# Keys of the first backward pass in two places of their own, and the first blocks of the projection in another order

## The chip, the cores and the metric

The kernel runs on one core of one Trainium2 chip. The metric is device time in microseconds (us). The kernel before took 2343.8 us, the median of three runs (2341.11 to 2347.96). The shares of busy time, the waits and the rows of the timeline come from one profiled execution of it.

The engines are called as in the profile: PE does the matmuls, PEld loads their stationary operand, DVE, ACT and POOL are the three engines that work on elements, SP issues the DMAs.

## The reference

One encoder layer on `x` of 2048 tokens by 1024 channels, all in float32. Cut to its steps:

```python
h = rms_norm(x, norm_pre_g)
proj = h @ w_in                       # 9232 columns
u_a, z_a, q, k, v, o, z_b, gates, g_a, g_b = split(proj)
pooled = multiscale_pool(u_a)         # branch A: windows 2, 4, 8, 16
y_a = (pooled @ pool_mix_w) * pool_scale * silu(z_a)
q, k = split(silu(centred_depthwise_conv(concat(q, k), conv_qk_w, conv_qk_b)))
...
# branch B: mLSTM, 4 heads of 256, both directions, chunks of 128 tokens
kw = kc * exp(w_end - m_chunk)        # weighted keys of one chunk
c_chunk = kw^T v                      # what the chunk adds to the state
c_new = keep * c_st + add * c_add     # the state, chunk after chunk
num = (q k^T * d) v + inter_scale * (q c_prev)
...
merged = sigmoid(g_a) * (y_a @ w_proj_pool) + sigmoid(g_b) * (y_b @ w_proj_mlstm)
out = x + rms_norm(merged @ w_out, norm_post_g)
```

## The kernel before

**Precision.** Nearly every matrix product is made of three matmuls (L110 to L112): each operand is split into a high part (`Copy` to the matmul's type on ACT, L98) and a low part (operand minus high part, on POOL or DVE, L102). The names end in `h` and `l`. `put` (L198) does that for a part of x, `prep_w` (L417) for a pair of blocks of weights.

**Phase 1** (L511) is the input projection, kept transposed: x in two halves of 1024 tokens, the columns of `w_in` in pairs of 2 x 128. For half 0, x is read as eight quarters `X[q]` of 128 x 2 x 512, scaled by the norm, and combined into the seven left operands of Strassen's scheme: A11, A12, A22 as they are, and S1 to S4, which `combos` (L206) makes from the four blocks a11, a12, a21, a22 **in place** (S1 lies where a22 was, S3 where a21 was, S2 where a11 was, S4 where a12 was). `operands` (L221) picks the room of each quarter (L227): `raw` and `acc` are rooms for working copies of the columns, `wc` is the pool of ten rooms in which the split blocks of weights lie, so two of those blocks (`wB`, `wT`) can be written only when the quarters in their rooms have been split.

The first two pairs of half 0 are made the plain way ("quarters", L500 to L502, 8 chunks of 128 channels, three matmuls each) while `combos` runs. Pair 2 is the first by Strassen's scheme (L443), in this order on PE: A11·B11 (bank A), S2·T2 (bank B), S1·T1 (bank C), S3·T3 (bank B again), A22·T4 and so on; T1 to T4 are sums of weight blocks. `u2` (L469) is bank B plus bank A's copy; S3·T3 goes into the same bank and so must wait for it. Between the products stand steps of other work: `pair_g` (L828) puts a sigmoid on a finished bank (`sg`, L841, ACT), `gates` (L658) sums the 16 gate columns and copies them out (`gsb`, L671, ACT), and `fps` (L373) are small matmuls that fold a weight of branch A.

**Ties.** The order on each engine is made by a scheduler from the order of the program and priorities. `tc.issue_after(x)` is a tie by hand: what is made under it stands behind `x` in the order. `prep_w` of pair 2 is tied so to `self.scaled[8]`.

**Fill-in matmuls.** `busy` (L277) is a matmul whose result nobody reads: one ahead of the sums of squares (`ssqp`, L258), one behind the broadcast of the norm's factor (`rbp`, L183).

**mLSTM** starts right behind phase 1. The first pass runs backwards over head 0: for the 16 chunks, `back1` (L1304) transposes the keys (`kt` on PE, L1311, copied to `kn` by ACT, L1314), `keys` (L1260) weighs them, and `update` (L1249) makes 15 states: two products `cu` of three matmuls (L1040 to L1042) per state, and on DVE the new state `cb` = old state times keep plus `cu` (L1256; the first is a copy by ACT, L1254). For the first pass alone the weighted keys take a way of their own: ACT makes `kw` (L1267) in a room of the pool `w1` (8 rooms, which otherwise carries weights of the output), DVE rounds it to the high part (CAST, L1268), POOL subtracts (L1269). All other passes use `weigh` (L1242): ACT writes the high part (L1244), DVE the low one in one instruction (L1245), in `KB` = 2 rooms per direction in the pool `io`. Behind each state the first outputs follow: `s` = q·k (L1374), its weights `dm` = Exp (L1377, ACT), `sd`, `qs`, and `num` (L1401 to L1406). Exp needs another table of functions in ACT than phase 1 uses; `none` (L1274) is an Exp of one column whose result nobody reads.

After that the passes of the heads, branch A, branch B and the output follow; nothing of the change lies there.

Of the kernel before, what the change touches and what calls it, by code (L numbers as in the profile page):

```python
# [8 lines left out]
F32 = mybir.dt.float32  # L9
F32R = mybir.dt.float32r  # L10
# [3 lines left out]
P = 128  # L14
# [67 lines left out]
class Kernel:  # L82
# [123 lines left out]
    def combos(self, H, j, a11, a12, a21, a22):  # L206

        nc = self.nc
        s1, s3, s2, s4 = a22, a21, a11, a12
        nc.vector.tensor_tensor(s1, a21, a22, op=ALU.add)  # L210
        nc.vector.tensor_tensor(s3, a11, a21, op=ALU.subtract)
        nc.vector.tensor_tensor(s2, s1, a11, op=ALU.subtract)
        self.put(H, "S2", j, s2, "act", "dve")
        self.put(H, "S1", j, s1, "act", "pool")
        self.put(H, "S3", j, s3, "act", "pool")
        return lambda: (
            nc.vector.tensor_tensor(s4, a12, s2, op=ALU.subtract),
            self.put(H, "S4", j, s4, "act", "dve"),
        )

    def operands(self, half, H, hp, wc, pool, psum):  # L221
# [5 lines left out]
        for b, q, where in ((0, 0, "raw"), (0, 2, "acc"), (0, 1, "acc"), (0, 3, "acc"), (1, 0, "raw"), (1, 2, "raw"), (1, 1, wc), (1, 3, wc)):  # L227
            if where is wc:
                t = wc.tile([P, 2, BLK], F32, tag="wc", name=self.nm("xT"))
            else:  # L230
                t = pool.tile([P, 2, BLK], F32, tag=where, name=self.nm("xT"))
            room[b, q] = t
# [15 lines left out]
        def sums():  # L248
# [8 lines left out]
            for i in range(4):  # L257
                nc.tensor.matmul(ps[:, i : i + 1], acc[:, i * P : (i + 1) * P], self.one_c, start=True, stop=True)  # L258
            busy(X[7][0][:, :P], X[7][0])
# [3 lines left out]
            busy(self.rstd[:, :1].to_broadcast([P, P]), X[7][0])  # L263
# [59 lines left out]
        ends = [self.combos(H, j, X[j][0], X[4 + j][0], X[j][1], X[4 + j][1]) for j in range(4)]  # L323
# [187 lines left out]
    def phase1(self):  # L511
        tc, nc, a = self.tc, self.nc, self.a
        with ExitStack() as es:
# [25 lines left out]
            for half in range(2):  # L539
# [53 lines left out]
                for i in range(2, n):  # L593
# [7 lines left out]
                    with tc.high_priority(offset=200):  # L601
                        if half == 0:
                            with tc.issue_after(self.scaled[8].ins) if i == 2 else ExitStack():
                                self.prep_w(W, load(i), wc, wt)
# [53 lines left out]
    def gates(self, half, H, W, psum, pool):  # L658
        nc = self.nc
        for b in range(2):  # L660
# [10 lines left out]
            nc.scalar.activation(g, ps, AF.Copy)  # L671
# [550 lines left out]
    def mlstm(self, turns, ends):  # L1222
        nc, tc, sp, col = self.nc, self.tc, self.sp, self.cols
        E = DH + 2
        with ExitStack() as es:
# [16 lines left out]
            def weigh(out, k, w):  # L1242

                nc.scalar.activation(out[0], k, AF.Copy, scale=w)  # L1244
                nc.vector.scalar_tensor_tensor(  # L1245
                    out[1], k, w, out[0].bitcast(F32), op0=ALU.mult, op1=ALU.subtract
                )

# [11 lines left out]
            def keys(h, c, d):  # L1260

                if d == 1 and h == 0:

                    kw = self.w1.tile([P, 2, 512], F32, tag="w", name=self.nm("kw"))[:, 0, :DH]
                    k = self.w1.tile([P, 2, 512], F32R, tag="w", name=self.nm("k"))
                    out = k[:, 0, :DH], k[:, 1, :DH]
                    up = nc.scalar.activation(kw, kn[h, c // 4][:, c % 4, :], AF.Copy, scale=col["w"][:, ix(d, h, c)])  # L1267
                    nc.vector.tensor_copy(out[0], kw)  # L1268
                    nc.gpsimd.tensor_tensor(out[1], kw, out[0].bitcast(F32), op=ALU.subtract)  # L1269
                    if c == NC_ // 2:  # L1270

                        none = last.tile([P, 1], F32, tag="none", name="none", bufs=1)
                        with tc.issue_after(up.ins):
                            nc.scalar.activation(none, self.one_c, AF.Exp)  # L1274
                    return out
                out = split2(io, [P, DH], f"k{d}", bufs=KB)
                weigh(out, kn[h, c // 4][:, c % 4, :], col["w"][:, ix(d, h, c)])
                return out
# [384 lines left out]
    def tail(self):  # L1663

        tc = self.tc
        with ExitStack() as es:
            w1 = self.w1 = es.enter_context(tc.tile_pool(name="w1", bufs=8, side="right", reuse_waits="tile"))
# [96 lines left out]
```

## Time and profile before

| | us |
|---|---|
| median of three runs | 2343.8 |
| the profiled execution | 2344.1 |
| its span, first to last instruction | 2342.3 |
| PE busy | 2285.9 (98% of the span) |
| mean granted TensorE clock | 0.993 |
| DVE / POOL / ACT busy | 1412.6 / 1184.2 / 885.8 |

Some 1.8 us of the profiled execution lie outside the span. PE is busy for nearly all of it and at the full clock nearly always, so what a change here can move is found by going through the stretches in which PE idles or has a lower clock, not by the shares of the whole. The busy time is of PE's matmuls, which overlap: the distance from start to start is the better measure of their rate.

### The profile page before, as it was taken

How to read it: one execution, taken by the hardware profiler on the slowest of the kernel's cores; microseconds unless marked ns; L12 is line 12 of the kernel's file. 1: busy time of each engine (PE TensorE's matmuls, PEld its weight loads, DVE VectorE, ACT ScalarE, POOL GpSimd, SP SyncE). 2: the span in 40 equal slices, each digit the busy share in tenths (PEclk: the TensorE clock that was granted, in tenths of full speed). 3: DMA queues.
4: the chain of work that ended last, by engine and by line, in shares of the span. 5: the costliest groups of instructions: out<-in, count | busy, mean ns of one | idle time of the engine just before them, and what ended most of it. 6: DMA issues, size and time to landing. Idle time of an engine off the chain costs nothing. (4 is left out here: it accounts for less than half of the span.)

```text
span 2342.3 us, 32965 instructions
## 1 busy us (share of the span) xinstructions
PE 2285.9 (98%) x11545; PEld 1938.1 (83%) x11545; DVE 1412.6 (60%) x2379; ACT 885.8 (38%) x1796; POOL 1184.2 (51%) x917
## 2 busy tenths in 40 slices
PE   7899999999999999999999999899999999999998
PEld 5788888888888788888878788699998888999886
DVE  6665656768765555546656565388887453454365
ACT  5334333333343423323333233467766221111342
POOL 4755545666664533356564555245556341233574
PEclk9999999999999999999999999899999999999999
DMA  5567766766685366788888787767767696677863
GB/s 211 188 237 271 259 222 223 265 234 219 222 296 206 110 203 212 228 297 279 295 298 287 265 299 270 258 193 246 238 190 243 219 321 227 214 277 256 329 207 126
DMA packets 233270, 564.43 MB, mean 241 GB/s; under 512 B 23568, under 2 KB 70800, under 8 KB 233104
## 3 DMA queue, kind: packets, MB, share of 16 engines
q1 hardware_dynamic: 233104, 562.33, 69.7%
q8 instruction: 91, 1.49, 0.3%
q14 instruction: 75, 0.61, 0.1%
HBM read 340.46 MB, written 221.77 MB: 240 GB/s over the span
## 5 line engine op out<-in xcount | busy, mean ns | idle before, releaser
L102 POOL TENSOR_TENSOR wB<-wraw,wB 128x512 fp32r<-128x512 f32 x220 | 333.1, 1518 | 293.3 <-ACT wB L98 232.7
L98 ACT ACTIVATE wB<-wraw 128x512 fp32r<-128x512 f32 x224 | 139.3, 626 | 268.7 <-PE bankB L112 121.9
L102 POOL TENSOR_TENSOR wT<-wt,wT 128x512 fp32r<-128x512 f32 x102 | 148.5, 1459 | 128.2 <-ACT wT L98 105.5
L718 DVE SCALAR_TENSOR_TENSOR acc<-raw,conv_w,acc 128x1026 f32<-128x1026 f32 (+1 forms) x96 | 151.2, 1587 | 10.5 <-ACT acc L713 9.7
L1040 PE MATMUL pb<-oxs,w_proj_mlstm 128*128 128x256 f32 x512 | 143.9, 281 | 0.7 <-DVE sga L1206 0.4
L1042 PE MATMUL pb<-oxs,w_proj_mlstm 128*128 128x256 f32 x512 | 143.9, 281 | 0.0
L1041 PE MATMUL pb<-oxs,w_proj_mlstm 128*128 128x256 f32 x512 | 143.8, 281 | 0.0
L98 ACT ACTIVATE wT<-wt 128x512 fp32r<-128x512 f32 x136 | 85.3, 629 | 153.5 <-PE bankB L112 60.4
L1385 POOL TENSOR_TENSOR qs<-q,isc 128x256 f32<-128x256 f32 x120 | 90.0, 754 | 93.1 <-PE num L1401 59.9
L110 PE MATMUL bankB<-S3h,wT 128*128 128x512 f32 x272 | 106.2, 390 | 3.6 <-DVE u L469 3.6
L110 PE MATMUL bankB<-A22h,wT 128*128 128x512 f32 x272 | 106.1, 390 | 2.1 <-DVE u L474 2.1
L110 PE MATMUL bankA<-A12h,wB 128*128 128x512 f32 x272 | 108.0, 397 | 0.0
L110 PE MATMUL bankC<-S4h,wB 128*128 128x512 f32 x272 | 106.2, 391 | 1.2 <-DVE raw L685 1.2
L112 PE MATMUL bankA<-A11h,wB 128*128 128x512 f32 x272 | 106.0, 390 | 1.3 <-POOL wB L102 1.3
L1025 POOL TENSOR_TENSOR nm<-nm,mask 128x256 f32<-128x256 f32 x64 | 60.4, 955 | 91.4 <-DMA nm<-negM 74.2
L111 PE MATMUL bankB<-S2l,wT 128*128 128x512 f32 x272 | 106.5, 392 | 0.0
L110 PE MATMUL bankC<-S1h,wT 128*128 128x512 f32 x272 | 106.4, 391 | 0.0
L111 PE MATMUL bankC<-S4l,wB 128*128 128x512 f32 x272 | 106.4, 391 | 0.0
L112 PE MATMUL bankA<-A12h,wB 128*128 128x512 f32 x272 | 106.2, 391 | 0.0
L110 PE MATMUL bankA<-A11h,wB 128*128 128x512 f32 x272 | 106.2, 390 | 0.0
L111 PE MATMUL bankA<-A12l,wB 128*128 128x512 f32 x272 | 106.1, 390 | 0.0
L112 PE MATMUL bankC<-S4h,wB 128*128 128x512 f32 x272 | 106.1, 390 | 0.0
(417 smaller groups left out, 7097.3 us busy)
## 6 DMA issues: line engine op xcount, KB each, us to landing
wt<-wT SPq DMA_DIRECT2D x136, 512.0 KB, 4.4
wT<-wt SPq DMA_DIRECT2D x136, 512.0 KB, 6.0
wraw<-in_w_in SPq DMA_DIRECT2D x98, 512.0 KB, 5.2
vh<-vnh SPq DMA_DIRECT2D x16, 516.0 KB, 4.4
vl<-vnl SPq DMA_DIRECT2D x16, 516.0 KB, 5.7
v<-vh SPq DMA_DIRECT2D x16, 516.0 KB, 8.8
v<-vl SPq DMA_DIRECT2D x16, 516.0 KB, 8.5
xT<-in_xT SPq DMA_DIRECT2D x16, 512.0 KB, 6.5
```

What stands on the lines that cost most here:

```text
L98: self.upper = nc.scalar.activation(hi, x, AF.Copy)
L102: return eng.tensor_tensor(lo, x, hi.bitcast(F32), op=ALU.subtract)
L110: nc.tensor.matmul(ps, wh, xh, start=start and kt == 0, stop=False, skip_group_check=True)
L111: nc.tensor.matmul(ps, wh, xl, start=False, stop=False, skip_group_check=True)
L112: end = nc.tensor.matmul(ps, wl, xh, start=False, stop=stop and kt == 3, skip_group_check=True)
L718: nc.vector.scalar_tensor_tensor(acc[:, :n], raw[:, tap : tap + n], self.cw[:, ct, tap : tap + 1], acc[:, :n], op0=ALU.mult, op1=ALU.add,)
L1025: nc.gpsimd.tensor_tensor(t[:, d, :, :], t[:, d, :, :], mask[:, d, None, :].to_broadcast([P, 2, P]), op=ALU.add)
L1040: nc.tensor.matmul(ps, wh, xh, start=i == 0, stop=False)
L1041: nc.tensor.matmul(ps, wh, xl, start=False, stop=False)
L1042: nc.tensor.matmul(ps, wl, xh, start=False, stop=i == n)
L1385: nc.gpsimd.tensor_tensor(qs[d], q[:, :, ck], isc[:, d, j % 2, None, :].to_broadcast([P, 2, P]), op=ALU.mult)
```

## The change

Three things at the start, two in the middle.

1. The rooms of the quarters of x: quarter (1,1), a half of a21, goes to a room `raw`, and quarter (1,2), a half of a22, to a room `wc` (before the other way round). Both rooms `wc` now hold a22, which becomes S1; before, one of them held a half of a21, which becomes S3. The low part of S1 of half 0 is made by DVE in place of POOL (4 instructions).
2. Fill-in matmuls: the first is tied behind the four `ssqp` and there are two behind `rbp` instead of one.
3. `prep_w` of pair 3 is tied behind the last `sg` and behind `gsb`.
4. The first pass's keys go through `weigh` like all others, in the two rooms of direction 1; the rooms in `w1`, the 15 CASTs on DVE and the 15 subtractions on POOL are gone, 15 `scalar_tensor_tensor` on DVE come in.
5. The Exp without a reader is tied, as before, behind the weighing of chunk 8.

```diff
-    def combos(self, H, j, a11, a12, a21, a22):
+    def combos(self, H, j, a11, a12, a21, a22, le):
...
-        self.put(H, "S1", j, s1, "act", "pool")
+        self.put(H, "S1", j, s1, "act", le)
...
-        for b, q, where in ((0, 0, "raw"), ..., (1, 0, "raw"), (1, 2, "raw"), (1, 1, wc), (1, 3, wc)):
+        for b, q, where in ((0, 0, "raw"), ..., (1, 0, "raw"), (1, 1, "raw"), (1, 2, wc), (1, 3, wc)):
...
-                nc.tensor.matmul(ps[:, i : i + 1], acc[:, i * P : (i + 1) * P], self.one_c, start=True, stop=True)
-            busy(X[7][0][:, :P], X[7][0])
+                done = nc.tensor.matmul(
+                    ps[:, i : i + 1], acc[:, i * P : (i + 1) * P], self.one_c, start=True, stop=True
+                )
+            with tc.issue_after(done.ins):
+                busy(X[7][0][:, :P], X[7][0])
...
-            busy(self.rstd[:, :1].to_broadcast([P, P]), X[7][0])
+            for _ in range(2):
+                busy(self.rstd[:, :1].to_broadcast([P, P]), X[7][0])
...
-        ends = [self.combos(H, j, X[j][0], X[4 + j][0], X[j][1], X[4 + j][1]) for j in range(4)]
+        ends = [self.combos(H, j, X[j][0], X[4 + j][0], X[j][1], X[4 + j][1], ("dve", "pool")[half]) for j in range(4)]
...
-                            with tc.issue_after(self.scaled[8].ins) if i == 2 else ExitStack():
+                            ties = [self.scaled[8]] if i == 2 else [self.evac, self.gated] if i == 3 else []
+                            with ExitStack() as behind:
+                                for t in ties:
+                                    behind.enter_context(tc.issue_after(t.ins))
                                 self.prep_w(W, load(i), wc, wt)
...
-            nc.scalar.activation(g, ps, AF.Copy)
+            self.gated = nc.scalar.activation(g, ps, AF.Copy)
...
             def keys(h, c, d):
-                if d == 1 and h == 0:
-                    kw = self.w1.tile([P, 2, 512], F32, tag="w", name=self.nm("kw"))[:, 0, :DH]
-                    k = self.w1.tile([P, 2, 512], F32R, tag="w", name=self.nm("k"))
-                    out = k[:, 0, :DH], k[:, 1, :DH]
-                    up = nc.scalar.activation(kw, kn[h, c // 4][:, c % 4, :], AF.Copy, scale=col["w"][:, ix(d, h, c)])
-                    nc.vector.tensor_copy(out[0], kw)
-                    nc.gpsimd.tensor_tensor(out[1], kw, out[0].bitcast(F32), op=ALU.subtract)
-                    if c == NC_ // 2:
-                        none = last.tile([P, 1], F32, tag="none", name="none", bufs=1)
-                        with tc.issue_after(up.ins):
-                            nc.scalar.activation(none, self.one_c, AF.Exp)
-                    return out
                 out = split2(io, [P, DH], f"k{d}", bufs=KB)
-                weigh(out, kn[h, c // 4][:, c % 4, :], col["w"][:, ix(d, h, c)])
+                up = weigh(out, kn[h, c // 4][:, c % 4, :], col["w"][:, ix(d, h, c)])
+                if (h, c, d) == (0, NC_ // 2, 1):
+                    none = last.tile([P, 1], F32, tag="none", name="none", bufs=1)
+                    with tc.issue_after(up.ins):
+                        nc.scalar.activation(none, self.one_c, AF.Exp)
                 return out
```

Line numbers of the kernel after run up to 8 higher from L281 on, and one lower behind `keys`; the rows below have their own.

PE's first rows, at the start of the program: `ssqp` are the sums of squares, `rbp` the broadcast, `bankA` and `bankB` the first products. Before:

```order
L281 MATMUL busy_352<-xT_310 128x512
L258 MATMUL ssqp_347<-one_c,sq_344 128x1 x4
L183 MATMUL rbp_357<-ident,rstd 128x128 x4
L281 MATMUL busy_363<-xT_310,rstd 128x512
L500 MATMUL bankA_504<-A11h_406,wB_35_394 128x512
```

And now:

```order
L258 MATMUL ssqp_347<-one_c,sq_344 128x1 x4
L285 MATMUL busy_352<-xT_310 128x512
L183 MATMUL rbp_357<-ident,rstd 128x128 x4
L285 MATMUL busy_363<-xT_310,rstd 128x512
L285 MATMUL busy_365<-xT_310,rstd 128x512
L504 MATMUL bankA_506<-A11h_408,wB_36_396 128x512
```

The first `busy` moved behind the four `ssqp`, and one more stands ahead of the first product.

ACT's rows in the middle of pair 2, from the last weights of pair 2 (`wT_94` and `wB_95` before) over the sigmoids of pair 1 to the copy of pair 2's first product (`p`); `wB_110` to `wB_117` are weights of pair 3. Before:

```order
L98 ACTIVATE wT_94_850<-wt_848 128x512
L98 ACTIVATE wB_95_853<-wraw_825 128x512
L841 ACTIVATE sg_781<-bankC_636,b_merge 128x512
L98 ACTIVATE wB_110_956<-wraw_952 128x512
L841 ACTIVATE sg_784<-bankC_637,b_merge 128x512
L98 ACTIVATE wT_113_963<-wt_961 128x512
L841 ACTIVATE sg_793<-bankA_644,b_merge 128x512
L98 ACTIVATE wT_114_966<-wt_959 128x512
L841 ACTIVATE sg_796<-bankB_645,b_merge 128x512
L671 ACTIVATE gsb_801<-gps_688 32x512
L98 ACTIVATE wT_116_971<-wt_969 128x512
L463 ACTIVATE p_101_877<-bankA_862 128x512
```

And now:

```order
L98 ACTIVATE wT_95_852<-wt_850 128x512
L98 ACTIVATE wB_96_855<-wraw_827 128x512
L848 ACTIVATE sg_783<-bankC_638,b_merge 128x512
L848 ACTIVATE sg_786<-bankC_639,b_merge 128x512
L848 ACTIVATE sg_795<-bankA_646,b_merge 128x512
L848 ACTIVATE sg_798<-bankB_647,b_merge 128x512
L678 ACTIVATE gsb_803<-gps_690 32x512
L98 ACTIVATE wB_111_958<-wraw_954 128x512
L98 ACTIVATE wT_114_965<-wt_963 128x512
L98 ACTIVATE wT_115_968<-wt_961 128x512
L98 ACTIVATE wT_117_973<-wt_971 128x512
L467 ACTIVATE p_102_879<-bankA_864 128x512
```

The four `sg` and `gsb` stand together ahead of pair 3's weights, between which they stood.

ACT's rows at the first pass, from the copies of the transposed keys (`kn`) on; `k` is a high part from `weigh`, `kw` the weighted key of the old way, `cb` the first state. Before, from the copies of the last whole group of four chunks:

```order
L1314 ACTIVATE kn_12081<-kt_12126 128x256
L1314 ACTIVATE kn_12081<-kt_12146 128x256
L1244 ACTIVATE k_1845_12202<-kn_12081,col_w 128x256
L1244 ACTIVATE k_1853_12221<-kn_12081,col_w 128x256
L1314 ACTIVATE kn_12163<-kt_12164 128x256
L1244 ACTIVATE k_1831_12168<-kn_12163,col_w 128x256
L1267 ACTIVATE kw_11838<-kn_11833,col_w 128x256
L1267 ACTIVATE kw_11847<-kn_11833,col_w 128x256
L1267 ACTIVATE kw_11867<-kn_11833,col_w 128x256
L1267 ACTIVATE kw_11887<-kn_11833,col_w 128x256
L1267 ACTIVATE kw_11910<-kn_11905,col_w 128x256
L1254 ACTIVATE cb_11852<-cu_11853 128x258
```

And now, from the last sigmoid of phase 1 (`u`):

```order
L848 ACTIVATE u_1717_11689<-u_1717_11689,b_merge 128x512
L1313 ACTIVATE kn_11835<-kt_11836 128x256
L1313 ACTIVATE kn_11835<-kt_11844 128x256
L1251 ACTIVATE k_1727_11840<-kn_11835,col_w 128x256
L1251 ACTIVATE k_1730_11848<-kn_11835,col_w 128x256
L1313 ACTIVATE kn_11835<-kt_11863 128x256
L1313 ACTIVATE kn_11835<-kt_11882 128x256
L1251 ACTIVATE k_1736_11867<-kn_11835,col_w 128x256
L1262 ACTIVATE cb_11852<-cu_11853 128x258
L1262 ACTIVATE cb_11852<-cu_11858 128x258
```

The weighing of the first chunk stood behind the copies of all 17 transposes and now stands behind two; the copies of later chunks come between the steps of the pass. On PE the first `cu` stood behind 17 `kt` in the same way and now stands behind four, and the first `s` stands behind the last `cu` of the pass, where before it stood behind the ninth. The load of Exp's table (before: ahead of the first `dm`) stands behind the key of chunk 8, the eighth of the 15.

More of the change, by code (lines that the diff above doesn't have):

```diff
@@ L226, in operands @@
         room = {}
-        for b, q, where in ((0, 0, "raw"), (0, 2, "acc"), (0, 1, "acc"), (0, 3, "acc"), (1, 0, "raw"), (1, 2, "raw"), (1, 1, wc), (1, 3, wc)):
+        for b, q, where in ((0, 0, "raw"), (0, 2, "acc"), (0, 1, "acc"), (0, 3, "acc"), (1, 0, "raw"), (1, 1, "raw"), (1, 2, wc), (1, 3, wc)):
             if where is wc:
@@ L1242, in weigh @@
             def weigh(out, k, w):
-                nc.scalar.activation(out[0], k, AF.Copy, scale=w)
+                up = nc.scalar.activation(out[0], k, AF.Copy, scale=w)
                 nc.vector.scalar_tensor_tensor(
@@ L1247, in weigh @@
                 )
+                return up
             def update(new, kw, v, old, keep):
@@ L1666, in tail @@
         with ExitStack() as es:
-            w1 = self.w1 = es.enter_context(tc.tile_pool(name="w1", bufs=8, side="right", reuse_waits="tile"))
+            w1 = es.enter_context(tc.tile_pool(name="w1", bufs=8, side="right", reuse_waits="tile"))
             self.kv = es.enter_context(tc.tile_pool(name="kv", bufs=KV, reuse_waits="tile"))
```

## Prediction

> **What bounds the kernel now.** I read the page's first part, then one table of windows over the whole span, then PE's waits in the two stretches that the table points to, then the timeline there.
>
> ```profile
> PE 2285.9 (98%) x11545; PEld 1938.1 (83%) x11545; DVE 1412.6 (60%) x2379; ACT 885.8 (38%) x1796; POOL 1184.2 (51%) x917
> ...
> core 0: us, PE busy (x) PEld busy (x) DVE busy (x) ACT busy (x) POOL busy (x), PEclk, DMA share, GB/s
> 0.00:20.40 20.40, 7.72 (x20) 4.49 (x20) 9.79 (x42) 10.44 (x17) 4.12 (x7) 1.00 0.92 318
> 20.40:24.90 4.50, 4.47 (x11) 3.51 (x12) 4.50 (x6) 3.48 (x10) 2.11 (x2) 1.00 1.02 415
> 24.90:74.90 50.00, 50.00 (x225) 38.85 (x223) 35.65 (x47) 24.45 (x47) 37.24 (x19) 1.00 0.22 80
> 74.90:95.70 20.80, 13.88 (x53) 10.85 (x52) 15.10 (x13) 11.66 (x23) 16.09 (x11) 0.84 0.78 273
> ...
> 1492.20:1508.20 16.00, 8.22 (x35) 4.74 (x33) 2.26 (x5) 9.02 (x23) 0.00 (x0) 0.62 1.04 410
> 1508.20:1516.50 8.30, 7.24 (x31) 6.95 (x32) 6.02 (x13) 7.22 (x18) 7.12 (x10) 0.50 0.76 265
> 1516.50:1532.00 15.50, 13.70 (x99) 12.54 (x99) 13.41 (x37) 6.23 (x15) 8.28 (x12) 1.00 0.85 295
> ```
>
> PE is the bound wherever it is full, as from 24.9 on: 50.00 of 50.00 us, 225 matmuls, one every 0.222 us. It is not full, or not at that rate, in three places: up to 24.9 (in 20.40 to 24.90 eleven matmuls in 4.5 us), from 74.9 to 95.7 (13.88 us busy of 20.8, clock 0.84), and at the first pass from 1492.2 to 1516.5 (clock 0.62, then 0.50) and on to 1532. All that the change touches lies there. Who ends PE's waits stands in brackets in the rows below.
>
> **The start, fill-in matmuls.** PE's timeline at the first products:
>
> ```profile
> 15.37 2.08 PE L183 MATMUL rbp<-ident,rstd 128*128 128x128 f32 x8 [1.74 <-POOL rstd L161]
> 17.24 1.91 PE L281 MATMUL busy<-xT,rstd 128*128 128x512 f32 x2
> 20.43 0.79 PE L500 MATMUL bankA<-A11h,wB 128*128 128x512 f32 x1 [1.27 <-ACT A11h L98]
> ```
>
> The eleven matmuls from 20.43 on start some 0.43 us apart (4.5 over 10.5), those after 24.9 every 0.222. That is ten at 0.21 us too much: **2.1 us of half clock** (the PEclk column, 1.00 there, doesn't show it; the count does). The change moves the first `busy` (1.9 us) into the hole ahead of `rbp` (15.37, a wait of 1.74) and adds one behind it, from 19.15 to about 21 at half clock, sooner if the clock has risen. PE is then busy with hardly a hole from 11.8 to 20.4, which is longer than the 4.5 us that it took from 20.43 on to bring the clock up. **Gain 2.1 us, bounds 0 and 2.1** (nothing, where fill-in work does not raise the clock; and an extra `busy` that ends at 21.0 instead of 20.43 would take 0.6 of it). The factor that `rbp` feeds comes through ACT and isn't touched.
>
> **The start, low half of S1 on DVE.** POOL's and DVE's rows while the plain pairs run, and what PE met behind them:
>
> ```profile
> 52.89 2.49 DVE L210 TENSOR_TENSOR xT<-xT,xT 128x512 f32<-128x512 f32 x4
> ...
> 54.32 14.99 POOL L102 TENSOR_TENSOR S1l<-xT,S1h 128x512 fp32r<-128x512 f32 x4 [3.71 <-ACT S1h L98]
> 69.27 5.95 POOL L102 TENSOR_TENSOR S3l<-xT,S3h 128x512 fp32r<-128x512 f32 x4
> 75.19 1.26 POOL L102 TENSOR_TENSOR wB<-wraw,wB 128x512 fp32r<-128x512 f32 x1
> ...
> 74.75 0.40 PE L111 MATMUL bankA<-A11l,wB 128*128 128x512 f32 x1
> 76.50 0.50 PE L112 MATMUL bankA<-A11h,wB 128*128 128x512 f32 x1 [1.34 <-POOL wB L102]
> ...
> 81.64 1.89 PE L373 MATMUL fps<-fm,fw 128*128 128x256 f32 x8
> 89.11 3.78 PE L373 MATMUL fps<-fm,fw 128*128 128x256 f32 x8 [5.57 <-ACT gsb L671]
> ```
>
> DVE's 19 instructions from 52.89 on take 0.60 us each (four in 2.49 with their overlap), without a hole to 64.4. POOL's four S1l took 15 us in the same time, where four S3l take 5.95: POOL hardly gets in while DVE runs so. Now DVE's stream has 25 instructions (4 S1l, the last S2l and one more come in): 52.9 + 25 x 0.60 = 68.0. POOL has only S3l: held up to 68.0, then 4 x 1.25 = 5 us, to 72.9, then the low part of B11 to 74.2 against 76.45 before. PE wants it at 74.97 (0.22 behind 74.75) and got on at 76.50. So this 1.5 us goes, by a margin of 0.8 us.
>
> Then `gsb`, ACT's last of a chain: the difference for T4 on DVE, its wT, wB, and four `sg` with three weights of pair 3 between them, one of which waited for DVE:
>
> ```profile
> 79.87 1.77 DVE L426 TENSOR_TENSOR wt<-wraw,wt 128x512 f32<-128x512 f32 x1
> ...
> 81.67 0.63 ACT L98 ACTIVATE wT<-wt 128x512 fp32r<-128x512 f32 x1 [3.18 <-DVE wt L426]
> ...
> 86.29 0.63 ACT L98 ACTIVATE wT<-wt 128x512 fp32r<-128x512 f32 x1 [1.79 <-DVE wt L426]
> ...
> 88.48 0.57 ACT L671 ACTIVATE gsb<-gps 32x512 f32<-32x512 f32 x1
> ```
>
> The tie puts these five together, 5 x 0.57 us behind wT and wB. The T4 difference needs T1's low part, POOL's next instruction behind B11's, so 74.2 + 1.2 = 75.4; at 1.7 us, as at 79.87 where DVE and POOL meet, it ends near 77, wT and wB near 78.1, `gsb` near **80.9**. PE reached the first `fps` at 81.64; without the 1.5 us it is there at 80.1 and at the second at 82.0. So the 5.57 us wait goes too, by a margin of 1 us, and with it the 8 `fps` at half clock (3.78 for 1.89) and the first S1·T1 at half clock.
>
> **What is late next.** S3·T3 must wait for `u2`, which stands on DVE behind differences for pairs 3 and 4:
>
> ```profile
> 85.67 0.33 SPq L346 DMA_DIRECT2D wraw<-in_w_in  x1
> ...
> 94.18 0.69 DVE L426 TENSOR_TENSOR wt<-wraw,wt 128x512 f32<-128x512 f32 x1 [2.19 <-DMA wraw<-in_w_in]
> 94.79 0.68 DVE L469 TENSOR_TENSOR u<-bankB,p 128x512 f32<-128x512 f32 x1
> ...
> 95.69 0.40 PE L110 MATMUL bankB<-S3h,wT 128*128 128x512 f32 x1
> ```
>
> Before, `u2` ended at 95.47 and bound nothing by much. Now PE wants S3·T3 at 82.0 + 1.89 + 2.7 (twelve products) = 86.6. From 52.9 on DVE and POOL have 36 and 12 instructions up to `u2`; where they exclude each other, that is 36 x 0.60 + 12 x 1.2 = 36 us, to 89.0, with `u2` near 89.7; the raw weight that stands ahead of it (94.18) was asked for at 85.67, behind POOL's weights of pair 2, and is now asked for some 3.5 us sooner. So a **new wait of about 3.1 us**, and S3·T3 starts at 89.7 against 95.69: **gain 6.0, bounds 4 and 9** (`u2` at 92, or no wait). Behind it the order is as before, and PE is full.
>
> Whether the clock survives that wait is open by these rows: a wait of 1.74 us at 1326 kept it (next starts 0.34 and 0.24 apart), one of 3.93 at 1226 lost it:
>
> ```profile
> 1230.13 1.76 PE L744 MATMUL vtr<-ident,raw 128*128 128x128 f32 x7 [3.93 <-DVE raw L685]
> ...
> 1327.75 0.50 PE L110 MATMUL bankB<-S3h,wT 128*128 128x512 f32 x1 [1.74 <-DVE u L469]
> ```
>
> Lost, it costs as at 20.43, 2.1 us. I take it as kept, since 1.4 above the kept one and 0.8 under the lost one leave it open, and give the other case to rival (1).
>
> The Trainium skill, page "TensorE: Matmul & The Clock Gate", section "Part 1: The HAM clock gate", has the clock fall after an idle window of about 3.4 us that runs free, and rise after as much of steady work. By that a wait of 3.1 us keeps the clock, and one of 3.5 loses it, and the sum is 2.1 us less. The waits of 1.74 and 3.93 us and the 4.5 us at 20.43 agree with it; no row here lies between.
>
> **The middle.** The first pass: three groups of lines over 1492 to 1532 (us busy, ns of one, idle before), then rows of the timeline:
>
> ```profile
> L1314 ACT ACTIVATE kn<-kt 128x256 f32<-128x256 f32 x20 | 7.3, 382 | 6.3 <-PE kt L1311 6.0
> L1244 ACT ACTIVATE k<-kn,col_w 128x256 fp32r<-128x256 f32 x4 | 1.9, 505 | 0.2
> L1245 DVE SCALAR_TENSOR_TENSOR k<-kn,col_w,k 128x256 fp32r<-128x256 f32 x4 | 1.9, 488 | 13.5 <-ACT k L1244 13.5
> ...
> 1505.78 0.66 PE L1311 MATMUL kt<-ident,kT 128*128 128x128 f32 x2 [2.30 <-DMA kT<-kT]
> ...
> 1508.23 0.58 PE L1040 MATMUL cu<-v,k 128*128 128x258 f32 x1 [1.79 <-DVE k L1268]
> ...
> 1517.01 0.29 PE L1041 MATMUL cu<-v,k 128*128 128x258 f32 x1
> 1517.13 0.28 PE L1042 MATMUL cu<-v,k 128*128 128x258 f32 x1
> ...
> 1527.06 4.47 DVE L1256 SCALAR_TENSOR_TENSOR cb<-cb,col_keep,cu 128x258 f32<-128x258 f32 x11
> ```
>
> Now PE does 17 transposes in 16 us, some of them waiting for DMAs of keys, before the first `cu` at 1508.23. In full clock `cu` start 0.12 us apart, so 96 `cu` are 11.6 us; transposes (42 at 0.11), scores (20 at 0.11) and `num` bring it to 19.2. Of 39.8 us from 1492.2 to 1532, **20.6 are lost**.
>
> After it, `cu` follows four transposes: 1492.2, `u` and two `kn` on ACT, two `k` and DVE's low part: the first `cu` near 1495. The period of a step is the largest of ACT (k 0.51 + kn 0.38 = 0.89), PE (6 x 0.12 + 2 x 0.11 = 0.94, at half clock 1.88), and DVE: one low part (0.49) and two `cb`, 0.41 us each in a row (eleven in 4.47 us), so 1.2 to 1.3. With handovers I take **1.35 us**, bounds 1.2 and 1.9. Fifteen steps are 20.3, plus 1.2 while the clock comes up, plus the table's 1.28 on ACT, which has 0.46 us of room a step, and a key ahead, and so hides it: the pass ends at 1517 with 16 us of PE's work done, 8.8 to 9.8 lost. The last group of keys had landed where PE stopped for one at 1505.78; by a period of 1.35 it is wanted at 1511. Then the hand-over to the outputs, `s`, `dm`, `sd`, `num` in a row, some 2.5 us lost, as no state work stands beside it. 12.3 against 20.6: **gain 8, bounds 3 and 13** (a period of 1.7 with 2.5 us of hand-over; 1.2 with none). The 15 CASTs and POOL's 15 subtractions go, DVE's 15 new instructions (0.49 each) come: time of engines that counts only through the period.
>
> The Trainium skill, page "ScalarE: Activation LUTs", section "What ACT_TABLE_LOAD costs", adds a drain of about 1.38 us to the load's 1.28. By that ACT would stand for 2.7 us in mid-pass and the sum would be 1.4 less, 2330. In the trace the next ACT instruction starts 0.02 us behind the load's end, so no drain behind it is seen here:
>
> ```profile
> 1511.31 1.28 ACT L1377 ACT_TABLE_LOAD   x1
> 1512.61 1.28 ACT L1377 ACTIVATE dm<-negM,col_a 128x128 f32<-128x128 f32 x4
> ```
>
> **Sum.** 2.1 + 6.0 + 8 = 16.1; I take off 0.6 for the second `busy` that may end after 20.43: 15.5. The profiled execution took 2344.1, the median is 0.3 below it, so the forecast is **2328.6 us**.
>
> **The rivals.** (1) The start gives back: the new wait before S3·T3 is longer (`u2` at 92) and loses the clock: 2.1 + 4 - 2.2 = 3.9, with the middle's 8 that is 2332; should the wake-up at 20.43 fail as well, 2334. For it: margins of 0.8 and 1 us, and an estimate for two engines that exclude each other. (2) The pass never leaves half clock, since PE is only 70% busy (0.94 of 1.35): 1.88 a step, 1495 + 28 = 1523, a gain of 2: 2334.5. Against it: at half clock PE would be full, and full PE got its clock after 4.5 us at 20.43. (3) The change does not do what it says: B11's low part and `gsb` are as late as before, since DVE and POOL hinder each other the same, and the pass waits for keys' DMAs: 2340 to 2344. (4) Slower: two places make the pass serial. A key's room is free only when PE has read it; if each step waited for its own key, `kn`, k, low part, `cu` at half clock and `cb` would stand in a row, 0.5 + 0.5 + 0.5 + 1.3 + 0.9 = 3.6 us a step, 54 us in all, 34 more than forecast: 2362. It decides from 1.9 us a step for the middle alone (8 / 15 over 1.35), from 2.4 for the whole (15.5 / 15). Against it: there are two rooms, and ACT's order has k two steps ahead of its `cu`.
>
> **How the numbers follow.** Forecast 0.62, rival (1) 0.14, (2) 0.11, (3) 0.08, (4) 0.05. The range takes the bounds of both gains, save their ends together (start 4 to 11, middle 3 to 13): 2320 to 2339, which holds the forecast, (1), (2) and the near edge of (3). The measurement of this kernel can tell some 0.3% (7 us) from no change. Faster than that, below 2336.8: forecast, nearly all of (1) and (2), 0.84. Within it 0.11, from (3) and the far edges of (1) and (2). Slower 0.05, from (4).
>
> **What would show it.** Right: products 0.23 us apart from the first one; no wait at B11's low part and at the second `fps`; a wait of 2 to 4 us before S3·T3, released by DVE's `u`; S3·T3 near 87.6 on the new clock of the trace (89.7 less 2.1); the first `cu` 3 us after phase 1, its steps 1.2 to 1.5 apart, PE's clock back to full within 5 us of it, the last of the pass 25 us after phase 1. Wrong: a step of over 1.9 us, a wait of `k` on PE's `cu` at every step, or a new wait in 20 to 96 that is longer than 4 us.

## The result and the profile after

| | before | after |
|---|---|---|
| median of six runs, us | 2346.14 | 2328.51 (2324.55 to 2330.54) |
| ratio, 95% interval | | 0.9926 (0.9913 to 0.9940) |
| the profiled execution's span | 2342.3 | 2327.6 |
| first S3·T3 | 95.69 | 89.35 |
| first `kt`, end of phase 1 | 1492.23 | 1491.04 |
| from there to the end | 850.1 | 836.6 |

The forecast of 2328.6 is met to 0.1 us. Part of that is chance: the kernel before ran at 2346.1 here, not at the 2343.8 of the runs ahead of the forecast, so the gain is 17.6 us by the medians where 15.5 was forecast. The last two rows say that it was met by the wrong sum as well: of the 14.7 us between the spans, 1.2 are won before the first pass and 13.5 in it and behind it. The forecast had 7.5 and 8.

The same windows as before (columns: us, then busy time and count of PE, PEld, DVE, ACT, POOL, then PEclk, DMA share, GB/s); the last is the first pass with the first outputs behind it (the pass's last `cb` ends at 1513.1):

```profile
20.40:24.90 4.50, 4.50 (x21) 3.73 (x20) 4.50 (x6) 4.50 (x14) 2.45 (x2) 1.00 1.01 408
24.90:74.90 50.00, 50.00 (x225) 38.97 (x225) 37.36 (x51) 26.40 (x49) 36.42 (x19) 1.00 0.26 92
74.90:95.70 20.80, 15.35 (x60) 12.28 (x59) 15.59 (x15) 9.34 (x19) 12.02 (x9) 0.84 0.94 334
...
1491.00:1517.20 26.20, 23.77 (x158) 20.06 (x157) 21.68 (x53) 19.79 (x52) 3.79 (x6) 1.00 1.01 356
```

From 20.4 to 24.9 PE now starts 21 matmuls where it started 11: full clock from the first products on. From 74.9 to 95.7 it starts 60 where it started 53, but the clock's column reads 0.84 as before. The first pass has lost its half clock: PEclk 1.00, where the three windows before had 0.62, 0.50 and 1.00.

PE's timeline of the kernel after, at pair 2:

```profile
77.52 3.62 PE L377 MATMUL fps<-fm,fw 128*128 128x256 f32 x16
...
89.35 0.80 PE L110 MATMUL bankB<-S3h,wT 128*128 128x512 f32 x1 [5.45 <-DVE u L473]
89.94 0.63 PE L111 MATMUL bankB<-S3l,wT 128*128 128x512 f32 x1
...
93.78 0.41 PE L111 MATMUL bankB<-S3l,wT 128*128 128x512 f32 x1
94.03 0.40 PE L112 MATMUL bankB<-S3h,wT 128*128 128x512 f32 x1
```

The 16 `fps` run in a piece, so the wait of 5.57 us between them is gone, and so is the one for B11's low part. One wait has come in their place: 5.45 us before S3·T3, for `u`. Behind it the ten products from 89.35 to 93.78 start 0.44 us apart, before the rate of 0.25 and less is back. That is the half clock again, some 2.1 us.

PE's groups of the kernel after over the 40 us from 1491.0 on (busy time, mean ns of one, idle before):

```profile
L1047 PE MATMUL cu<-v,k 128*128 128x258 f32 x45 | 15.0, 337 | 0.8 <-DVE cb L1264 0.4 <-DVE cf L1264 0.3
L1049 PE MATMUL cu<-v,k 128*128 128x258 f32 x44 | 13.1, 305 | 0.0
L1048 PE MATMUL cu<-v,k 128*128 128x258 f32 x44 | 12.3, 283 | 0.0
L1310 PE MATMUL kt<-ident,kT 128*128 128x128 f32 x44 | 8.0, 278 | 1.6 <-ACT kn L1313 1.6
L1400 PE MATMUL num<-cb,qs 128*128 128x258 f32 x16 | 4.1, 380 | 0.0
L1373 PE MATMUL s<-q,kT 128*128 128x128 f32 x24 | 3.5, 274 | 0.0
L1403 PE MATMUL num<-v,sd 128*128 128x258 f32 x8 | 3.5, 434 | 0.0
L1400 PE MATMUL num<-cf,qs 128*128 128x258 f32 x12 | 3.1, 380 | 0.0
```

Busy times overlap, so I count starts: 133 `cu` and 24 `num` from v at 0.12 us, 44 `kt` and 24 `s` at 0.11, and 28 `num` from the states at 0.217 (their distance when they follow one another) make some 32.5 us of work (32.4 by these rounded distances). **7.5 of 40 us are lost; before, by the same count, 20.6.** In the rest of this text "lost" is this figure. By 140 us it is 8.6 against 22.6: before, a later wait of 1.3 us for DVE is in it that is gone as well.

### The profile page after: what moved, and what is told of

The parts are those of the page before. It is cut to its first block, busy times and chain, and to the rows that moved or that the text cites. A ratio compares the mean times of both kernels' runs of the same rounds, so it can differ in the third digit from the quotient of the medians.

```text
span 2327.6 us, 32973 instructions
## 1 busy us (share of the span) xinstructions
PE 2281.5 (98%) x11547; PEld 1934.6 (83%) x11547; DVE 1418.7 (61%) x2383; ACT 884.5 (38%) x1796; POOL 1168.4 (50%) x898
## 5 line engine op out<-in xcount | busy, mean ns | idle before, releaser
L110 PE MATMUL bankB<-S3h,wT 128*128 128x512 f32 x272 | 107.8, 396 | 9.9 <-DVE u L473 9.9
L430 DVE TENSOR_TENSOR wt<-wraw,wt 128x512 f32<-128x512 f32 x68 | 64.7, 952 | 74.6 <-POOL wT L102 56.8
L111 PE MATMUL bankB<-S3l,wT 128*128 128x512 f32 x272 | 107.3, 394 | 0.0
L112 PE MATMUL bankB<-S3h,wT 128*128 128x512 f32 x272 | 107.3, 394 | 0.0
L110 PE MATMUL bankA<-A11h,wB 128*128 128x512 f32 x272 | 106.2, 390 | 0.0
```

What stands on the lines that cost most here:

```text
L110: nc.tensor.matmul(ps, wh, xh, start=start and kt == 0, stop=False, skip_group_check=True)
L111: nc.tensor.matmul(ps, wh, xl, start=False, stop=False, skip_group_check=True)
L112: end = nc.tensor.matmul(ps, wl, xh, start=False, stop=stop and kt == 3, skip_group_check=True)
L430: nc.vector.tensor_tensor(t, x, y, op=ALU.subtract)
```

## The experiments

Each of the three groups had its own runs of the kernel before on its chip; times (medians, with the number of runs) are compared within a group only, and between groups by their ratios to before. "Wait" is PE's before S3·T3.

| kernel | group | time, us | S3·T3 | wait | first `kt` | `kt` to end |
|---|---|---|---|---|---|---|
| before | 1 | 2344.3 (15 runs) | 95.69 | none | 1492.23 | 850.1 |
| keys only | 1 | 2327.34 (5) | 94.77 | none | 1488.55 | 837.0 |
| start only | 1 | 2340.76 (11) | 89.54 | 5.4 | 1490.39 | 852.1 |
| behind u2 | 1 | 2317.26 (4) | 83.53 | none | 1477.55 | 836.1 |
| no tie | 1 | 2330.13 (1) | 91.28 | none | 1492.03 | 836.3 |
| before | 2 | 2340.66 (1) | | | | |
| S1 on POOL | 2 | 2325.25 (1) | 90.85 | 3.9 | 1485.86 | 837.6 |
| old fill-ins | 2 | 2321.47 (1) | 88.93 | 5.5 | 1484.27 | 835.4 |
| one place | 2 | 2329.73 (1) | 89.13 | 5.4 | 1489.15 | 838.8 |
| more on DVE | 2 | 2329.17 (1) | 89.20 | 5.4 | 1489.03 | 838.4 |
| before | 3 | 2341.42 (7) | | | | |
| u2 tie alone | 3 | 2318.57 (4) | 84.34 | none | 1481.08 | 835.4 |
| u2, S1 on POOL | 3 | 2320.57 (4) | 87.19 | 0.3 | 1485.24 | 836.3 |
| no early table | 3 | 2326.6 (1) | 89.61 | 5.5 | 1486.78 | 838.1 |
| no fill-ins | 3 | 2328.2 (1) | 92.05 | 5.4 | 1488.02 | 838.4 |

### The two halves apart

The first kernel has the new keys of the first pass (parts 4 and 5 of the change) and the old start; the second has the new start and the old keys.

> The kernel before with the keys of the first pass (and the early Exp) as changed, the start as before. Theory A (the parts are independent; the first pass is worth its 13.1 us of lost PE time, 20.6 before and 7.5 after): 13 to 14 us faster than before, about 2332; the wait of 5.6 us for gsb near 84 stays. Theory B (the prediction's sizes, 8 us): 2338. Theory C (the middle profits because phase 1 ends earlier and DMAs stand otherwise): under 6 us, over 2340.

> The kernel after with the keys of the first pass as before; the start as changed. Theory A: PE is 4 us earlier than before at 230 us, and loses up to 3 of it again near 1325 (a longer wait for DVE's u, and the clock): 1 to 4 us faster than before, 2342 to 2345. Theory B (the prediction's 7.5 us): 2338.5. The wait before S3*T3 near 84 is 5 to 6 us and loses the clock.

Ratios to before: keys only 0.9930 (0.9917 to 0.9942), that is 16.4 us (13.6 to 19.5); start only 0.9991 (0.9980 to 1.0002), that is 2.1 us (from 0.5 slower to 4.7 faster). The keys alone give what the whole change gives (0.9926); what the start adds can't be told from nothing by the times. The profiles agree: from the first `kt` to the end the kernels with old keys take 850.1 and 852.1 us, the others, the start being old or new, 835.4 to 838.8.

Two things stay open here. The 16.4 us are more than the 13.1 that the profiles show behind the first `kt` (850.1 against 837.0): in its one profile "keys only" is ahead by another 3.7 us at the first `kt`, with a start that is the same code as before. Single profiles scatter by that much there, as is shown below. And within the new keys, their place in the order and their way through the engines (no room of `w1`, no CAST, no POOL) were not tried apart.

### What makes u2 late

DVE and ACT in the kernel after, just ahead of `u` (`wt` are differences of weights, `wT` their high parts, `p` the copy of bank A that `u` needs):

```profile
85.28 1.74 DVE L430 TENSOR_TENSOR wt<-wraw,wt 128x512 f32<-128x512 f32 x1 [1.17 <-POOL wT L102]
87.06 1.64 DVE L430 TENSOR_TENSOR wt<-wraw 128x512 f32<-128x512 f32 x1
88.62 0.68 DVE L473 TENSOR_TENSOR u<-bankB,p 128x512 f32<-128x512 f32 x1
```

```profile
82.75 1.67 ACT L98 ACTIVATE wT<-wt 128x512 fp32r<-128x512 f32 x3 [3.54 <-DVE wt L430]
84.33 0.58 ACT L467 ACTIVATE p<-bankA 128x512 f32<-128x512 f32 x1
```

PE had the last product of bank C behind it at 83.9. `u` started 4.7 us later: on DVE it stood behind weights of the pairs that follow, which nobody needs yet, and `p` stood on ACT behind three `wT` that waited for DVE. So the wait is one of order, and a tie should take it away. Pair 3's `prep_w` was tied behind the reading of bank B by `u2` too (`read_banks[0]`), at first beside the change's own ties, then in their place:

```diff
-ties = [self.scaled[8]] if i == 2 else [self.evac, self.gated] if i == 3 else []
+ties = [self.scaled[8]] if i == 2 else [self.evac, self.gated, self.read_banks[0]] if i == 3 else []
```

> The kernel after with one more tie: the weights of pair 3 also stand behind u2 of pair 2, so that u2 comes on DVE right behind the last S4l. Theory A (the wait before S3*T3 is the queue on ACT and DVE ahead of u2, the weights of pairs 3 and 4): no wait before S3*T3, no lost clock, PE 7 us earlier at 96 us; the time 4 to 7 us below the kernel after. Theory B (u2 is late since DVE and POOL exclude each other, whatever the order): the wait stays over 3 us and the time is the same. Theory C: the wait comes back at pair 3, whose weights are later: same time.

Its DVE and its PE at the same place:

```profile
74.46 6.84 DVE L102 TENSOR_TENSOR S4l<-xT,S4h 128x512 fp32r<-128x512 f32 x4
81.23 0.68 DVE L473 TENSOR_TENSOR u<-bankB,p 128x512 f32<-128x512 f32 x1
```

```profile
83.31 0.39 PE L112 MATMUL bankC<-S1h,wT 128*128 128x512 f32 x1
83.53 0.39 PE L110 MATMUL bankB<-S3h,wT 128*128 128x512 f32 x1
```

`u` runs 7.4 us sooner, S3·T3 follows the product before it by 0.22, and the clock holds (products 0.23 apart). This version is the best of all: ratio 0.9887 (0.9872 to 0.9903), 10 us below the kernel with the new keys alone in the same group. Its interval lies below that of the kernel after (0.9913 to 0.9940), so it beats both kernels of this case.

The next has that tie alone, `[self.read_banks[0]] if i == 3`:

> The kernel of e6 without the ties to the last sg and to gsb: pair 3's weights stand behind u2 alone. Only ACT's order differs, one weight comes between the first two sg. Theory A (u2 is the tie that counts): S3*T3 within 1 us of e6's 83.5, the time within 2 us of e6's 2317. Theory B (the change's ties are needed as well): a wait for gsb of 2 us or more at the second fps and S3*T3 later by as much.

0.9912 (0.9893 to 0.9931), S3·T3 at 84.34 with no wait. Its interval overlaps that of the version with all three ties, so the change's own ties are not seen to add anything once `u2` is tied. It overlaps that of the kernel after as well; here it is the trace that shows the gain. At PE's first transpose `vtr` (242.14 before) this kernel is 11.3 us ahead of before, the one with all three ties 11.9, the kernel after 3.9. Without any tie of pair 3 (`ties = [self.scaled[8]] if i == 2 else []`):

> The kernel after without the tie of pair 3's weights. Theory A (the tie alone takes the wait for gsb away, with POOL free earlier): a wait of 3 to 5 us before the second fps comes back, and the wait before S3*T3 shrinks by as much, so that S3*T3 starts at 88 to 91 as with the tie (89.35): the tie only moves the wait. Theory B (the tie is worth its whole wait): S3*T3 starts later by 3 us or more.

PE's only large wait of that kernel at pair 2:

```profile
PE fps L377 <- ACT gsb L678: 6.2, 1, 6.2
```

The wait for `gsb` is back, the one for `u` is gone, and S3·T3 is 1.9 us later than in the kernel after. By 225 us nothing is left of that: the last S2 product ahead of the next wait ends at 225.38 there, at 225.68 in the kernel after. The change's tie moves the wait from `gsb` to `u`; it removes little of it.

### S1's low part, and the rooms

POOL makes the low part of S1 again, with the rooms as before; the ties are the change's:

```diff
-for b, q, where in (..., (1, 0, "raw"), (1, 1, "raw"), (1, 2, wc), (1, 3, wc)):
+for b, q, where in (..., (1, 0, "raw"), (1, 2, "raw"), (1, 1, wc), (1, 3, wc)):
...
-ends = [self.combos(H, j, ..., ("dve", "pool")[half]) for j in range(4)]
+ends = [self.combos(H, j, ..., "pool") for j in range(4)]
```

> The kernel after with S1's low part of half 0 on POOL again and the rooms of x as before; fill-ins, tie and keys as after. Theory A (POOL gets in only behind DVE's stream, so eight low parts end 5 us later than four): B11's low part about 5 us later than in the kernel after (71.7 there), a wait of 1 to 2 us of PE at it near 73, gsb later than the fps want it by 1 to 3 us. Theory B (the move to DVE changes nothing, since POOL is free either way by then): PE's rows up to 84 as in the kernel after within 0.5 us.

PE's waits at pair 2 of this kernel:

```profile
PE bankB L110 <- DVE u L473: 3.9, 1, 3.9
PE fps L377 <- ACT gsb L678: 1.4, 1, 1.4
PE bankB L112 <- DVE wT L102: 0.7, 1, 0.7
```

S3·T3 is 1.5 us later. PE comes to it 3.0 us later (86.93 against 83.90; two waits are back, for `gsb` and for a low part of T2) and waits 1.5 less there: half of what the new room plan gives is spent in that wait. So it was tried where the wait is gone, with the tie behind `u2`:

> The kernel of e6 (pair 3's weights also behind u2) with S1's low part on POOL and the rooms of x as before. Theory A (the queue ahead of u2 is all that is late, S1's engine is worth the 1 to 1.5 us of e4): S3*T3 at 84 to 86 (83.5 in e6), the time 1 to 2 us above e6's 2317. Theory B (with u2 early, POOL's eight low parts are the next bound): waits of PE at B11's low part or gsb add up to 3 us or more, S3*T3 at 87 or later, about 2321 or more.

S3·T3 at 87.19 against 83.53: here the new rooms with S1 on DVE are worth 3.7 us at that place; which of the two, was not tried. In both kernels with S1 on POOL the two engines took turns (last section), so a run in which they don't could give another figure. By the times, 0.9914 (0.9898 to 0.9930) stands against the 0.9887 (0.9872 to 0.9903) of the kernel from which it differs by this alone, in another group: the intervals just meet.

### The fill-in matmuls

First the fill-ins of before in the new kernel, then none at all (their results are read by nobody):

> The kernel after with the fill-in matmuls of before (one ahead of the sums of squares, one behind the broadcast of the norm's factor). Theory A (the fill-ins raise the clock before the first product): the first products start 0.43 us apart for some 4.5 us and everything up to 70 us is 2.1 us later than in the kernel after. Theory B (the clock is up for another reason, such as the phase of its window in that run): spacing 0.23 from the first product, nothing later by more than 0.5 us.

> The kernel after with no fill-in matmul at all at the start. Theory A (the fill-ins bring the clock up): the first products 0.43 us apart for 4 us or more, DVE's stream and S3*T3 later by about 2 us than in the kernel after (50.4 and 89.35). Theory B (the sums of squares and the broadcast alone bring it up, or the phase of the clock's window decides): spacing 0.23 within 2 us of the first product.

PE's first products, with the old fill-ins:

```profile
19.59 0.50 PE L501 MATMUL bankA<-A11h,wB 128*128 128x512 f32 x1 [0.60 <-ACT A11h L98]
19.92 0.40 PE L502 MATMUL bankA<-A11h,wB 128*128 128x512 f32 x1
```

and without any:

```profile
20.10 0.80 PE L500 MATMUL bankA<-A11h,wB 128*128 128x512 f32 x1 [2.64 <-ACT A11h L98]
20.70 0.63 PE L501 MATMUL bankA<-A11h,wB 128*128 128x512 f32 x1
21.12 0.63 PE L500 MATMUL bankB<-A11h,wB 128*128 128x512 f32 x1
```

With none, 13 products run at half rate, to 25.8, and S3·T3 is 2.7 us later. With the old ones the clock was full here; in the two other profiles with old fill-ins (before and keys only) it was half. With the new ones all ten profiles have full rate from the second product on. The records of the granted clock in the traces say the same: it turned to full at 16.5 to 19.5 us in the ten, at 18.73 with the old fill-ins here, and at 24.93, 24.50 and 25.79 in before, "keys only" and "no fill-ins". So fill-in work does raise the clock, and the new places gave in ten of ten profiles what the old ones gave in one of three.

"Old fill-ins" is also the fastest kernel of its group, by 3.8 us, and its first `kt` comes 4.8 us ahead of the one of "more on DVE". That is not won at the fill-ins: at 100 us it is 4.4 us ahead of before, the kernel after 4.1. It is won behind 242 us, in code that is the same in both, and is a measure of the scatter of a single run.

### The middle

**One place** for the keys of direction 1, in all passes, in place of two (`bufs=KB - d`), to see whether the number of places can bind:

> The kernel after with one place for the keys of direction 1 instead of two, in all passes. Theory A (two places are what lets the pass run at DVE's 1.18 us a step; with one, k waits for cu, and k, low part and cu stand in a row, 0.5 + 0.5 + 0.7 and their hand-overs): 1.8 to 2.2 us a step in the first pass, 9 to 15 us more loss there (7.5 in the kernel after), and later passes partly hidden; 2340 or more. Theory B (places don't matter while DVE is the bound): under 1.4 us a step.

Its waits over the pass (total, times, longest):

```profile
PE cu L1049 <- DVE k L1252: 1.6, 5, 0.5
...
PE cu L1047 <- ACT k L1251: 1.3, 4, 0.6
```

Now `cu` does wait for keys, in nine places: 1.91 us a step (from the first to the last of the pass's 28 `cb` on DVE, 13.5 steps) and 13.3 us lost, against 1.26 and 7.5. From the first `kt` to the end, though, it costs only 2.2 us (838.8 against 836.6). The loss is still 5 us larger 140 us on (13.5 against 8.6); where later some of it is made good wasn't followed, and kernels that are alike behind phase 1 scatter by 3 us in this figure.

**More on DVE**: one copy (0.28 us, read by nobody) behind every key's low part of the first pass.

```diff
+if (h, d) == (0, 1):
+    more = last.tile([P, DH], F32, tag="more", name=self.nm("more"), bufs=1)
+    nc.vector.tensor_copy(more, kn[h, c // 4][:, c % 4, :])
```

> The kernel after with one more instruction on DVE per step of the first pass, a copy of the key (128x256) that nobody reads. Theory A (DVE sets the period: 0.40 a low part and two times 0.40 a state): the step goes from 1.18 to 1.18 plus the copy's 0.2 to 0.4 us, 3 to 6 us more loss in the pass. Theory B (ACT or the two places set it): the step stays within 0.1 us of 1.18.

A step takes 1.46 us, 0.19 more, and where DVE has no hole 1.39 against 1.18: DVE sets the step. The loss is 8.6 against 7.5, 1.1 more and less than the 3 that fifteen such steps would add. PE had the half clock for 3.4 us of this pass (from 1507.7 on, `cu` 0.21 us apart), so even the 1.1 need not be the copies' alone. The whole from the first `kt` is 1.8 us longer, less than these kernels scatter.

**No early table**: the Exp without a reader is left out.

> The kernel after without the Exp whose result nobody reads, so that ACT loads the table ahead of the first dm, behind the first pass. Theory A (in mid-pass ACT has room and the load is hidden; behind the pass it stands in the hand-over): from the first transpose to the end 1.0 to 1.5 us more than in the kernel after (836.6 there, 835.4 to 837.6 in its kin). Theory B (the hand-over has other work on PE and hides it as well): within 0.5 us.

ACT of this kernel, and then of the kernel after:

```profile
1509.48 1.28 ACT L1371 ACT_TABLE_LOAD   x1
1510.78 1.28 ACT L1371 ACTIVATE dm<-negM,col_a 128x128 f32<-128x128 f32 x4
```

```profile
1500.84 1.28 ACT L1276 ACT_TABLE_LOAD   x1
1502.13 0.20 ACT L1276 ACTIVATE none<-one_c 128x1 f32<-128x1 f32 x1
```

The load goes to the first `dm`; at 100 us it makes the loss 8.8, against 8.1 in the kernel after and 8.3 with the keys alone. From the first `kt` to the end it takes 1.5 us longer (838.1 against 836.6), which lies inside the scatter of 3 us. A cost of half a us or so is all that shows, which a single run can't settle.

## Why the forecast came out right

**Fill-ins, 2.1 less 0.6: right, and the 0.6 was not needed.** First product at 20.05, not later than before; full rate from the second on, so that the 21st starts 2.5 us sooner; without fill-ins 2.7 us later at S3·T3.

**Low half of S1 and `gsb`: right by the result.** `gsb` ended at 78.69, forecast 80.9 less the 2.1 of the earlier start; neither old wait is left. What takes them away is less sure. The wait for B11's low part (1.34 us) is missing in "keys only" too: it has the old start, but there POOL took turns with DVE (last section) and was done with S1 and S3 at 67.4 us instead of 75.2; 0.7 us for a low part of T2 stand in its place. And `gsb`'s wait is 6.2 us without the tie and 1.4 with the tie and S1 on POOL, so the tie does most of it.

**The new wait before S3·T3: the place was right, the term too small, and the clock wrong.** Forecast: 3.1 us, clock kept, a gain of 6.0 at that place. Measured: 5.45 us, clock lost. PE arrived 0.6 us sooner than thought (83.9 against 86.6 less 2.1), and `u` ended at 89.3, not 87.6: POOL had 14 instructions, not 12, to get in between DVE's, and DVE stood 1.17 us for one of them. By the forecast's own list a wait of over 4 us here was a sign of being wrong, and rival (1) came true. S3·T3 starts 6.3 us earlier than before, 2.1 of which are the fill-ins' and 2.1 of which the half clock takes again: 3.9 us are left at 242 us (238.21 against 242.14), which is rival (1)'s sum for the start. The failed step is "I take it as kept", and the sum of 36 and 12 instructions beneath it. By the last section a wait of 3.1 us keeps or loses the clock by where it falls, and one of 5.45 loses it in any case. What the forecast didn't ask is whether the wait must be: one more tie removes it.

**From there to the end of phase 1: not in the forecast.** In the kernel after 4.1 us were still won at 1226, and 1.2 at 1491. Most of the difference is lost in one place. PE waits near 1325 for `u`, and two rows of the kernel after, of POOL and of DVE, show what held it:

```profile
1313.47 0.74 POOL L1032 TENSOR_TENSOR nm<-nm,mask 128x256 f32<-128x256 f32 x1 [5.62 <-DMA nm<-negM]
```

```profile
1316.13 6.25 DVE L782 TENSOR_TENSOR win<-win 128x1044 f32<-128x1044 f32 x3 [1.90 <-POOL win L782]
```

POOL stood 5.62 us for a DMA of `negM`, its part of `win` came late by that, DVE stood 1.90 for it, and `u` (1324.25) stands four instructions behind `win`. PE's wait there was 1.74 us before, clock kept, and 2.92 after, clock lost. "More on DVE" and "one place" have the same instructions there and waited 1.38 and 1.03, "behind u2" not at all. In all fourteen profiles this `u` starts 10.76 to 10.79 us behind that `nm`, wherever PE is, so PE's wait follows from when that DMA lands and when PE arrives. What moves the landing against PE, no run here varied alone.

It is one of several such places, and together they hide the start's gain. The five kernels with this start (after, "start only", "one place", "more on DVE", "no early table") are 3.9 to 4.6 us ahead of before at 100 us, 2.1 to 5.2 at 242 us and 1.2 to 5.4 at the first `kt`. "Keys only", with the old start, is 0.9, 0.6 and 3.7 us ahead. So some 4 us are won at the start, and at the end of phase 1 they can't be told from the scatter.

**The middle, 8: right in kind, too small by 5 to 8.** The first `cu` came 2.64 us behind the first `kt` (forecast: 3). Three terms of the remaining loss were too big, 7.5 against 12.3 in all. The clock never fell, as PE's transposes and `cu` run on from phase 1 without a long hole (waits of 1.6 us in two pieces): the 1.2 us for its rise weren't needed. The step was 1.26 us, not 1.35; where DVE has no hole it is 1.18, three instructions of 0.395:

```profile
1508.30 0.48 DVE L1252 SCALAR_TENSOR_TENSOR k<-kn,col_w,k 128x256 fp32r<-128x256 f32 x1
1508.70 0.88 DVE L1264 SCALAR_TENSOR_TENSOR cb<-cb,col_keep,cu 128x258 f32<-128x258 f32 x2
1509.48 0.48 DVE L1252 SCALAR_TENSOR_TENSOR k<-kn,col_w,k 128x256 fp32r<-128x256 f32 x1
```

And the hand-over to the outputs, put at 2.5 us, is nearly free: of the 7.5 us, 6.0 are lost in the first 20 us and 1.4 in the next ten. The first `s` starts at 1513.99, 2 us behind the last `cu` of the pass, with transposes and `cu` of the next pass to fill in around it. The forecast had "no state work stands beside it"; it does. That DVE is the bound of the step was right ("more on DVE" shows it), and rival (4), a pass made serial by its places, is real in kind with one place (1.91 us a step, not 3.6) and not with two. The last 1.3 us are the later wait for DVE, which the forecast had not looked at.

**So two errors cancel.** By the times the middle alone gives 16.4 us (13.6 to 19.5) where the forecast had 8, and the start 2.1 (−0.5 to 4.7) where it had 7.5. A forecast of 2328.6 that rests on those two terms was right by luck; each half alone would have been forecast wrongly.

## What to carry to other kernels

A stretch in which one chain of small steps feeds PE is worth most when the work of its start is put between the steps: here that kept PE from a long hole, and with the hole went the half clock. When a wait is removed, ask at once who is next and what stands in front of that one on its engine; here one further tie put PE 8 us further ahead at 242 us; by the times the start gave some 10 us with it, and without it 2, which can't be told from nothing. And a forecast that fits in sum is not yet right: time each half by itself.

## What the runs showed of the hardware

**The clock after a wait.** PE of the kernel after, at the wait near 1325:

```profile
1324.99 0.50 PE L110 MATMUL bankB<-S3h,wT 128*128 128x512 f32 x1 [2.92 <-DVE u L473]
...
1325.79 0.43 PE L110 MATMUL bankB<-S3h,wT 128*128 128x512 f32 x1
1326.02 0.63 PE L111 MATMUL bankB<-S3l,wT 128*128 128x512 f32 x1
```

Four products start at full rate, and only then do they go to 0.43 us apart: the loss shows 1 us after the wait is over. With "no tie" a wait of 1.86 us lost the clock in the same way, while "one place" kept it over one of 3.17:

```profile
227.24 0.50 PE L110 MATMUL bankB<-A22h,wT 128*128 128x512 f32 x1 [1.86 <-DVE u L478]
...
228.06 0.58 PE L110 MATMUL bankB<-A22h,wT 128*128 128x512 f32 x1
228.44 0.63 PE L111 MATMUL bankB<-A22l,wT 128*128 128x512 f32 x1
228.86 0.63 PE L112 MATMUL bankB<-A22h,wT 128*128 128x512 f32 x1
```

```profile
229.00 0.50 PE L110 MATMUL bankB<-A22h,wT 128*128 128x512 f32 x1 [3.17 <-DVE u L478]
229.34 0.40 PE L111 MATMUL bankB<-A22l,wT 128*128 128x512 f32 x1
...
230.50 0.39 PE L110 MATMUL bankB<-A22h,wT 128*128 128x512 f32 x1
```

Waits of 1.86, 2.02, 2.35, 2.36, 2.92, 3.9 and 5.45 us lost the clock; 1.74, 2.13, 2.63 and 3.17 kept it. Between 1.8 and 3.2 us the length alone doesn't decide.

The records of the granted clock in the traces show what does. In each of the fourteen traces all changes of the clock lie on one grid of 3.413 us, to 0.01 us, from the first, at 16 to 26 us, to the last, at 2310 to 2339; the half clock lasts one step of it or several (3.41 us at 1326 in the kernel after, 20.48 in the first pass before). Cut phase 1 behind 20 us along that grid, and add up PE's idle time in each step that ran at full clock. The clock fell behind each of the 30 steps with 1.87 us or more, and behind none with 1.84 or less, 72 of which had over 0.6. So the 3.17 us kept the clock because they lay in two steps, 1.71 and 1.45 us in each, and the 1.86 lost it because they lay in one. By this a wait of over 3.7 us, twice 1.85, can't be kept wherever it lies. This holds for phase 1 with its long products: in the first pass of "more on DVE" a step with 1.11 us of idle lost the clock. The Trainium skill, page "TensorE: Matmul & The Clock Gate", section "Part 1: The HAM clock gate", speaks of an activity window of about 3.4 us that runs free of the program. The grid of 3.413 us agrees with such a window; that only an idle time of 3.4 us loses the clock doesn't agree with the 1.86.

**POOL beside DVE.** The four S1l on POOL, the same code, in the kernel with the new keys alone:

```profile
53.82 6.72 POOL L102 TENSOR_TENSOR S1l<-xT,S1h 128x512 fp32r<-128x512 f32 x4 [3.70 <-ACT S1h L98]
```

6.72 us, against 14.99 in the trace of before (and 6.74 and 6.71 in the two other kernels that have them on POOL), while in the kernel after four S3l took 16.04:

```profile
54.41 16.04 POOL L102 TENSOR_TENSOR S3l<-xT,S3h 128x512 fp32r<-128x512 f32 x4 [6.27 <-ACT S3h L98]
```

Either POOL is held for as long as DVE has work, or the two take turns at some 1.7 us each; which of the two comes about differs from run to run for the same code (before and "keys only" have the same start). With S1 on DVE, POOL was held in all ten kernels (16.03 to 16.05 us). A price of one instruction read from one trace holds for the one case only.
